# First down projection of a two-layer trunk: the B21 rows stay in SBUF, and the A12 chunks take over their buffers

## The chip, the cores and the metric

The kernel runs on one core of one Trainium2 chip. The metric is device time in microseconds (us) of one execution. Three runs before the change gave 2187.07, 2189.74 and 2186.4 us; the median is 2187.07 us.

## The reference

Two layers over 1024 tokens of width 1024, all float32. Layer 0 has an attention mixer, layer 1 a recurrent one, and each ends with a SwiGLU block. What this case touches is the end of layer 0's SwiGLU block and the start of layer 1's recurrent block:

```python
def swiglu(h, w_gate, w_up, w_down):
    return (jax.nn.silu(h @ w_gate) * (h @ w_up)) @ w_down
...
        f = swiglu(h, ffn_w_gate[layer], ffn_w_up[layer], ffn_w_down[layer])   # w_down: 2816 x 1024
        x = x + rmsnorm(f, norm_ffn_post[layer])
...
        h = rmsnorm(x, norm_mix_pre[layer])                 # of the next layer
    proj = h @ w_in                                         # recurrent_mixer: 1024 x 2048
    gate, xr = jnp.split(proj, 2, axis=-1)
```

## The kernel before

**Numbers.** Each float32 operand of a matmul is split into two fp32r parts, `hi` (a cast on ScalarE, ACT) and `lo` (source minus `hi`, on VectorE, DVE), and each product is three matmuls: hi·hi, hi·lo, lo·hi. A cast and a subtraction thus stand ahead of every operand of TensorE (PE).

**The down stage** (`down`, run once for each layer) multiplies the 1024 x 2816 activations by `w_down` with a seven-product scheme on 2 x 2 blocks. The inner dimension is cut in 11 steps, j = 0 to 10 (`NP`), of two row blocks of 128. The block row 1 of `w_down` at step j has a left half, B21, and a right half, B22. The products run in the order p1, p6, p7, p5, p4, p3, and last A12·B21. Each of the first six is 11 steps of 4 x 3 matmuls of 128 x 512 into four banks `ps`. The last is done in four **units** a = 0 to 3, each of 33 matmuls into one bank: a unit gives one group of 128 rows.

- p4 needs B21 once, to form an operand (`t4`), and the units need it again.
- p3 loads two halves of a `raw` buffer (3 buffers) for each step: S4 (a result of the stage before, stored in DRAM) and B22, and splits both: S4 into a buffer of the tag `w` (8 buffers), B22 into `wb` (4).
- The units' left operand, A12, comes in three **chunks** of 4, 4 and 3 steps for each unit, so 12 chunks, each loaded from DRAM into a buffer `act` (2 buffers) and split into a buffer `wb`.

**The norms.** After p4 four groups of rows (r = 1, a = 0 to 3; the result tiles `m2`) are complete, and after each unit one more (r = 0; `m1`). For each one a chain runs: squares on ACT (`junk`), an inverse root on GpSimd (POOL, `rs`), scaling and adding to x on DVE, squares of x on ACT, another root on POOL, scaling on ACT, then a **turn**: eight 128 x 128 transposes on PE, written in two banks `pst`, from which ACT casts `hi` and DVE subtracts `lo` into `hT`, the next stage's right operand.

**The next stage** (`recurrent`) starts with `xr([0, 1, 2])`: three 1024 x 128 pieces of `rg_w_in` are loaded into `raw`, scaled by a gain on DVE, and split into two `w` buffers each (`whi`, `wlo`). Their matmuls take first the tokens of half 0 of `hT`, then half 1. The next pieces (c = 3 and 4) are scaled on POOL, eight instructions each.

**Order.** The code is written for a tile framework that follows every buffer and puts the instructions of each engine in an order by its own estimate of the time; `behind` (which calls `issue_after`) forces an instruction to be placed after a named one. On the chip each engine takes its queue strictly in that order: an instruction that waits holds all behind it. SP's queue issues nearly all DMAs in this part of the program. A buffer of a tag with n buffers is reused n allocations later, and its new writer waits for the last reader of the old content.

The second layer's `down` runs the same code with `keep` true; there B21 and B22 stay in the buffers `ts`.

Of the kernel before, what the change touches and what calls it, by code (L numbers as in the profile page):

```python
# [8 lines left out]
F32 = mybir.dt.float32  # L9
# [3 lines left out]
ALU = mybir.AluOpType  # L13
PSUM = bass.MemoryType.PSUM

P = 128
# [83 lines left out]
class Trunk:  # L100
# [36 lines left out]
        self.last_load = self.nc.sync.dma_start(raw.rearrange("p (a b) -> p a b", a=a), src).ins  # L137
        return raw

    def split(self, src, a, b, gain=None, raw=None, pool=False):  # L140

        nc, m = self.nc, self.main
        if raw is None:
            raw = self.raw(src, a)
        if gain is not None and pool:
            for i in range(a):
                v = raw[:, i * b:(i + 1) * b]
                nc.gpsimd.tensor_scalar(v, v, gain[:, i:i + 1], 1.0, op0=ALU.mult, op1=ALU.mult)
        elif gain is not None:
            v = raw.rearrange("p (a b) -> p a b", a=a)  # L150
            nc.vector.tensor_tensor(v, v, gain.rearrange("p (a o) -> p a o", o=1).to_broadcast([P, a, b]),
                                    op=ALU.mult)
        hi = m.tile([P, 1024], F32R, tag="w", bufs=8, name=self.uid("whi"))
        lo = m.tile([P, 1024], F32R, tag="w", bufs=8, name=self.uid("wlo"))
        nc.scalar.copy(hi, raw)  # L155
        nc.vector.tensor_tensor(lo, raw, hi.bitcast(F32), op=ALU.subtract)  # L156
        return (hi.rearrange("p (a b) -> p a b", a=a),
                lo.rearrange("p (a b) -> p a b", a=a))
# [657 lines left out]
    def down(self, l, gO, x_src, x_dst, make_sink):  # L816
# [4 lines left out]
        nc, io = self.nc, self.io  # L821
        w = io["ffn_w_down"][l]
        NP = NF // 2
        tt = nc.vector.tensor_tensor

        def block(j, row, c0=0, n=D):
            return w[(2 * j + row) * P:(2 * j + row + 1) * P, c0:c0 + n]

        def split(pool, tag, bufs, src):
            t = pool.tile([P, 2, 512], F32R, tag=tag, bufs=bufs, name=self.uid("o"))  # L830
            nc.scalar.copy(t[:, 0], src)  # L831
            tt(t[:, 1], src, t[:, 0].bitcast(F32), op=ALU.subtract)  # L832
            return t

        def matmuls(ps, a, b, first, last):
            nc.tensor.matmul(ps, a[0], b[:, 0], start=first, stop=False)  # L836
            nc.tensor.matmul(ps, a[0], b[:, 1], start=False, stop=False)  # L837
            nc.tensor.matmul(ps, a[1], b[:, 0], start=False, stop=last)  # L838

        def product(operands, first=0):  # L840
            ps = [self.psum() for _ in range(4)]
# [8 lines left out]
        main = self.main  # L850

        keep = make_sink is nullcontext
        with self.pool(f"d{l}") as ap, ExitStack() as right:
# [12 lines left out]
            def fetch(name, j, src=None):  # L866
                r = main.tile([P, 2, 512], F32, tag="raw", bufs=3, name=self.uid("raw"))
                self.mark = nc.sync.dma_start(r[:, 0], gO[name][j]).ins
                if src is not None:
                    nc.sync.dma_start(r[:, 1], src)  # L870
                return r[:, 0], r[:, 1]
# [25 lines left out]
            def p5(j):  # L897
# [2 lines left out]
                    self.load(ts[j][:, 0], block(j, 1, 0, 512))  # L900
                return sp(a), sp(ts[j][:, 1])

            def p4(j):
                a, t4 = fetch("A22", j, None if keep else block(j, 1, 0, 512))
                tt(t4, ts[j][:, 2], ts[j][:, 0] if keep else t4, op=ALU.subtract)
                if keep:
                    self.load(ts[j][:, 1], block(j, 1, 512, 512))
                return sp(a), sp(t4)
# [15 lines left out]
            with make_sink() as sink:  # L924
                def norm(r, a, m):
                    ms, mg = [(slice(0, D), m)], m
                    if r == 0 and sink is None:
                        ms = [(c, m[:, c]) for c in (hi, lo)]
                        mg = ap.tile([P, D], F32, tag="mg", bufs=1, name=self.uid("mg"))

                    x = main.tile([P, D], F32, tag="raw", bufs=3, name=self.uid("x")) if keep and r == 0 else None
                    self.post_norm(ms, mg, x_src, x_dst, (r, a), gpost, sink, ap, x)

                for a in range(4):
                    norm(1, a, m2[a])

                def p3(j):
                    r = main.tile([P, 2, 512], F32, tag="raw", bufs=3, name=self.uid("raw"))
                    nc.sync.dma_start(r[:, 0], gO["S4"][j])
                    b22 = ts[j][:, 1]  # L940
                    if not keep:
                        b22 = r[:, 1]
                        nc.sync.dma_start(b22, block(j, 1, 512, 512))
                    return split(main, "w", 8, r[:, 0]), split(ap, "wb", 4, b22)

                for m, ps in zip(m1, product(p3)):
                    tt(m[:, hi], ps, m[:, hi], op=ALU.add)
                b21 = []
                for j in range(NP):
                    if keep:  # L950
                        src = ts[j][:, 0]
                    else:
                        if j % 2 == 0:
                            r = main.tile([P, 2, 512], F32, tag="raw", bufs=3, name=self.uid("raw"))
                        src = r[:, j % 2]
                        nc.sync.dma_start(src, block(j, 1, 0, 512))
                    b21.append(split(*((main, "w", 8) if j < 6 else (ap, "wc", 5)), src))
                for a in range(4):
                    ops = []
                    for j in range(0, NP, 4):  # L960
                        n = min(4, NP - j)
                        r = ap.tile([P, 4, P], F32, tag="act", bufs=2, name=self.uid("act"))[:, :n]
                        self.load(r, gO["A12"][:, j:j + n, a * P:(a + 1) * P])
                        t = ap.tile([P, 2, 4, P], F32R, tag="wb", bufs=4, name=self.uid("o"))
                        nc.scalar.copy(t[:, 0, :n], r)  # L965
                        tt(t[:, 1, :n], r, t[:, 0, :n].bitcast(F32), op=ALU.subtract)  # L966
                        ops += [(t[:, 0, i], t[:, 1, i]) for i in range(n)]
                    ps = self.psum()
                    for j in range(NP):
                        matmuls(ps, ops[j], b21[j], j == 0, j == NP - 1)  # L970
                    tt(m1[a][:, lo], ps, m1[a][:, lo], op=ALU.add)
                    norm(0, a, m1[a])
        self.mark = None


    def recurrent(self, ap, hT, yT):
# [21 lines left out]

        psum = self.psum

        def w_load(c0, pool=True):

            return self.split(w_in[:, c0:c0 + P].rearrange("(k p) c -> p k c", p=P), KT, P, self.gcol[:, 2],
                              pool=pool)

        def act(*a, **k):

# [9 lines left out]

        def xr(cs):

            ws = {c: w_load(1024 + c * P, len(cs) == 1) for c in cs}  # L1020
            carry = {c: ap.tile([P, 3], F32, tag="carry", bufs=4, name=self.uid("carry")) for c in cs}
            for c in cs:
                xcs[c] = [ap.tile([P, S], F32, tag="xc", bufs=4, name=self.uid("xc"))]
# [237 lines left out]
```

## Time and profile before

| | us |
|---|---|
| median of three runs | 2187.07 |
| the profiled execution | 2190.47 |
| its span, first to last instruction | 2188.7 |
| PE busy | 2160.6 (99%) |
| DVE busy | 1502.0 (69%) |
| ACT busy | 1171.6 (54%) |
| PE waits between 1150 and 1243 us, in which p3 and the units lie | 4.7 |

The span is the time between the first and the last instruction; the profiled execution's own time is 1.8 us longer. PE is called busy while a matmul is anywhere in its pipeline. A 128 x 512 matmul is in it for 0.39 us while the next one starts 0.227 us later, so a gap below 0.16 us does not show as a wait, and the loss is better read from the starts of matmuls. Lines (L837) are those of the kernel before; a line such as L831 (`hi`) or L832 (`lo`) belongs to a helper that all products share.

### The profile page before, as it was taken

The numbers are of one execution on the slowest core, as the hardware profiler recorded it, in microseconds if no ns is written. First come the engines' busy times: TensorE is split into PE (matmuls) and PEld (weight loads), VectorE is DVE, ScalarE is ACT, GpSimd is POOL, SyncE is SP. The second block draws the span as 40 slices with busy tenths as digits, with TensorE's granted clock in tenths as the row PEclk, the third lists the DMA queues.
The fourth block names the chain that finished last, engine by engine and source line by source line (L and its number), as shares of the span: only waits on it lengthen the run. The fifth ranks groups of instructions, "written<-read, shape, count | busy, mean of one in ns | idle before, by whom it ended". The sixth has DMA issues, their size and how long they took to land.

```text
span 2188.7 us, 30464 instructions
## 1 busy us (share of the span) xinstructions
PE 2160.6 (99%) x11140; PEld 1803.1 (82%) x11140; DVE 1502.0 (69%) x2458; ACT 1171.6 (54%) x2174; POOL 210.3 (10%) x398
## 2 busy tenths in 40 slices
PE   9999999999999999999999999999999999999998
PEld 8898989878788888888887777888788888888886
DVE  4747555556877677767768678437786767758675
ACT  6656555556855545433446676538755454424453
POOL 2111113121100000000002333102100000000011
PEclk9999999999999999999999999999999999999999
DMA  7111011126334233336468411356233333328565
GB/s 284 44 40 59 30 38 56 45 93 216 135 98 138 92 121 96 112 100 242 135 194 241 128 57 39 110 189 228 76 131 101 122 96 102 106 87 292 169 182 155
DMA packets 169039, 272.32 MB, mean 124 GB/s; under 512 B 14140, under 2 KB 95036, under 8 KB 168888
## 3 DMA queue, kind: packets, MB, share of 16 engines
q1 hardware_dynamic: 168248, 268.27, 38.3%
q10 hardware_dynamic: 640, 2.10, 0.3%
q8 instruction: 87, 1.43, 0.3%
q14 instruction: 64, 0.52, 0.1%
HBM read 202.69 MB, written 65.54 MB: 123 GB/s over the span
## 4 chain that ended last, share of the span: by engine, by line
PE 88%; DVE 4%; DMA 3%; ACT 2%; issue 2%; POOL 0%; SPq 0%; POOLq 0%; ACTq 0%; DVEq 0%
PE ps L752 13%; PE ps L753 13%; PE ps L751 13%; PE ps L594 7%; PE ps L837 5%; PE ps L838 5%; PE ps L836 5%; PE pso L366 3%; PE tr L431 3%; PE psq L166 3%; PE psq L167 2%; PE psq L168 2%; PE ps L166 2%; PE ps L167 2%; PE ps L168 2%
## 5 line engine op out<-in xcount | busy, mean ns | idle before, releaser
L752 PE MATMUL ps<-hS,q 128*128 128x512 f32 (+1 forms) x1288 | 489.8, 380 | 0.5 <-DVE hS L89 0.5
L751 PE MATMUL ps<-hS,q 128*128 128x512 f32 (+1 forms) x1288 | 490.0, 381 | 0.0
L753 PE MATMUL ps<-hS,q 128*128 128x512 f32 (+1 forms) x1288 | 489.3, 380 | 0.0
L722 DVE TENSOR_TENSOR q<-raw,q 128x512 fp32r<-128x512 f32 x308 | 205.6, 687 | 175.1 <-ACT q L721 174.3
L752 PEld LDWEIGHTS ps<-hS,q 128*128 128x128 f32 x1288 | 242.9, 189 | 47.1 <-DVE hS L89 0.9
L751 PEld LDWEIGHTS ps<-hS,q 128*128 128x128 f32 x1288 | 242.5, 189 | 46.4 <-DVE tf L89 0.5
L753 PEld LDWEIGHTS ps<-hS,q 128*128 128x128 f32 x1288 | 243.0, 189 | 45.6
L721 ACT CAST q<-raw 128x512 fp32r<-128x512 f32 x308 | 178.7, 616 | 172.5 <-DVE raw L730 116.9
L837 PE MATMUL ps<-o,o 128*128 128x512 f32 x616 | 240.2, 390 | 0.6 <-DVE o L832 0.6
L838 PE MATMUL ps<-o,o 128*128 128x512 f32 x616 | 237.9, 390 | 0.3 <-DVE o L966 0.3
L836 PE MATMUL ps<-o,o 128*128 128x512 f32 x616 | 221.6, 391 | 3.5 <-ACT o L965 3.0
L709 ACT ACTIVATE raw<-raw,gcol 128x256 f32<-128x256 f32 x352 | 150.4, 498 | 131.2 <-DMA raw<-in_ffn_w_up_dram 73.2
L831 ACT CAST o<-raw 128x512 fp32r<-128x512 f32 x184 | 110.3, 620 | 161.7 <-PE ps L838 49.4
L182 POOL TENSOR_SCALAR rs<-ss 128x1 f32<-128x1 f32 x52 | 25.2, 484 | 1420.3 <-ACT junk L178 1355.8
L832 DVE TENSOR_TENSOR o<-raw,o 128x512 fp32r<-128x512 f32 x184 | 123.5, 689 | 54.4 <-ACT o L831 53.7
L836 PEld LDWEIGHTS ps<-o,o 128*128 128x128 f32 x616 | 115.4, 188 | 30.5 <-ACT o L965 5.1
L837 PEld LDWEIGHTS ps<-o,o 128*128 128x128 f32 x616 | 115.7, 188 | 25.8 <-DVE o L832 2.1
L838 PEld LDWEIGHTS ps<-o,o 128*128 128x128 f32 x616 | 115.6, 188 | 24.8 <-DVE o L966 1.2
L156 DVE TENSOR_TENSOR wlo<-raw,whi 128x1024 fp32r<-128x1024 f32 x76 | 93.6, 1231 | 57.4 <-ACT whi L155 56.3
L419 DVE TENSOR_TENSOR_SCAN pr<-pr,zero 128x128 f32<-128x128 f32 (+7 forms) x64 | 86.6, 1358 | 51.3 <-POOL pr L416 49.6
L155 ACT CAST whi<-raw 128x1024 fp32r<-128x1024 f32 x76 | 79.7, 1049 | 48.5 <-PE ps L167 19.9
L166 PE MATMUL psq<-hT,whi 128*128 128x512 f32 x256 | 102.3, 400 | 0.2 <-DVE st L337 0.2
(206 smaller groups left out, 4263.8 us busy)
## 6 DMA issues: line engine op xcount, KB each, us to landing
raw<-in_ffn_w_gate_dram SPq DMA_DIRECT2D x44, 512.0 KB, 4.2
raw<-in_ffn_w_up_dram SPq DMA_DIRECT2D x44, 512.0 KB, 4.2
gS<-c SPq DMA_DIRECT2D x88, 256.0 KB, 3.7
raw<-gS SPq DMA_DIRECT2D x88, 256.0 KB, 2.9
gA<-c SPq DMA_DIRECT2D x66, 256.0 KB, 3.3
raw<-in_ffn_w_down_dram SPq DMA_DIRECT2D x63, 256.0 KB, 4.4
raw<-gA SPq DMA_DIRECT2D x44, 256.0 KB, 2.8
t<-in_ffn_w_down_dram SPq DMA_DIRECT2D x22, 512.0 KB, 6.6
```

The costliest lines, as they stand in the source:

```text
L166: nc.tensor.matmul(ps, wh[:, kt, cols], hh[:, kt, :], start=kt == 0, stop=False)
L594: self.matmul = nc.tensor.matmul(ps[:, n * 512:(n + 1) * 512], x, y[:, n, :], start=first and i == 0, stop=last and i == len(passes) - 1).ins
L709: nc.scalar.activation(raw[:, i], raw[:, i], AF.Copy, scale=gain[:, 4 * k + i:4 * k + i + 1])
L721: self.last = nc.scalar.copy(t[:, 0], src).ins
L722: self.last_lo = nc.vector.tensor_tensor(t[:, 1], src, t[:, 0].bitcast(F32), op=ALU.subtract).ins
L751: nc.tensor.matmul(ps, a[:, 0, kt, :], bh, start=kt == 0, stop=False)
L752: nc.tensor.matmul(ps, a[:, 0, kt, :], bl, start=False, stop=False)
L753: self.matmul = nc.tensor.matmul(ps, a[:, 1, kt, :], bh, start=False, stop=kt == 3).ins
L832: tt(t[:, 1], src, t[:, 0].bitcast(F32), op=ALU.subtract)
L836: nc.tensor.matmul(ps, a[0], b[:, 0], start=first, stop=False)
L837: nc.tensor.matmul(ps, a[0], b[:, 1], start=False, stop=False)
L838: nc.tensor.matmul(ps, a[1], b[:, 0], start=False, stop=last)
```

## The change

Only the first `down` and the start of `recurrent` change in what they do; the second `down` keeps its order on every engine.

1. In p4 the B21 rows go into 11 buffers `act` of their own and stay there. The 11 loads of B21 after p3 go away. Steps 0 to 4 are split inside p3's steps (into `wc`, 5 buffers), steps 5 to 10 after p3 (into `w`). Before, steps 0 to 5 went into `w` and 6 to 10 into `wc`.
2. The 12 A12 chunks take the same 11 buffers, each as soon as the B21 rows in it are split.
3. The turns are held. The norms are started as before, but their transposes are placed by hand: three of r = 1 at the steps 5, 7 and 9 of p3, the fourth and then those of r = 0 behind step 7 of units 0, 2 and 3, the last two behind unit 3.
4. The gain scaling of the first three `rg_w_in` pieces, c = 0, 1, 2, is placed behind the last split of unit c + 1.

```diff
-    def split(self, src, a, b, gain=None, raw=None, pool=False):
+    def split(self, src, a, b, gain=None, raw=None, pool=False, behind=()):
...
-            nc.vector.tensor_tensor(v, v, gain.rearrange("p (a o) -> p a o", o=1).to_broadcast([P, a, b]),
-                                    op=ALU.mult)
+            with self.behind(behind):
+                nc.vector.tensor_tensor(v, v, gain.rearrange("p (a o) -> p a o", o=1).to_broadcast([P, a, b]),
+                                        op=ALU.mult)
...
+            b21 = []
+
+            def small():
+                return ap.tile([P, 512], F32, tag="act", bufs=2 if keep else NP, name=self.uid("act"))
+
+            def split_b21(j, src):
+                return split(*((main, "w", 8) if (j < 6 if keep else j >= 5) else (ap, "wc", 5)), src)
+
             def p4(j):
-                a, t4 = fetch("A22", j, None if keep else block(j, 1, 0, 512))
-                tt(t4, ts[j][:, 2], ts[j][:, 0] if keep else t4, op=ALU.subtract)
+                a, t4 = fetch("A22", j)
+                b21.append(ts[j][:, 0] if keep else small())
+                if not keep:
+                    self.load(b21[j], block(j, 1, 0, 512))
+                tt(t4, ts[j][:, 2], b21[j], op=ALU.subtract)
...
-                    self.post_norm(ms, mg, x_src, x_dst, (r, a), gpost, sink, ap, x)
-
-                for a in range(4):
-                    norm(1, a, m2[a])
+                    return self.post_norm_of(ms, mg, x_src, x_dst, (r, a), gpost, sink, ap, x)(True)
+
+                turns = [norm(1, a, m2[a]) for a in range(4)]
+
+                def turn():
+                    if not keep:
+                        with self.behind([self.matmul]):
+                            turns.pop(0)()()
 
                 def p3(j):
+                    if j in (5, 7, 9):
+                        turn()
...
+                        if j < 5:
+                            b21[j] = split_b21(j, b21[j])
...
-                for j in range(NP):
-                    if keep:
-                        src = ts[j][:, 0]
-                    else:
-                        if j % 2 == 0:
-                            r = main.tile([P, 2, 512], F32, tag="raw", bufs=3, name=self.uid("raw"))
-                        src = r[:, j % 2]
-                        nc.sync.dma_start(src, block(j, 1, 0, 512))
-                    b21.append(split(*((main, "w", 8) if j < 6 else (ap, "wc", 5)), src))
+                for j in range(0 if keep else 5, NP):
+                    b21[j] = split_b21(j, b21[j])
...
-                        r = ap.tile([P, 4, P], F32, tag="act", bufs=2, name=self.uid("act"))[:, :n]
+                        r = small().rearrange("p (n b) -> p n b", n=4)[:, :n]
...
+                    self.units.append(self.last_lo)
...
                         matmuls(ps, ops[j], b21[j], j == 0, j == NP - 1)
+                        if j == 7 and a != 1:
+                            turn()
                     tt(m1[a][:, lo], ps, m1[a][:, lo], op=ALU.add)
-                    norm(0, a, m1[a])
+                    turns.append(norm(0, a, m1[a]))
+                if not keep:
+                    for t in turns:
+                        t()()
...
-            ws = {c: w_load(1024 + c * P, len(cs) == 1) for c in cs}
+            ws = {c: w_load(1024 + c * P, len(cs) == 1, () if len(cs) == 1 else self.units[c + 1:c + 2]) for c in cs}
```

How this moves instructions is shown at three places. The order's own line numbers are used: a line of the kernel after stands one to some twenty lines further down (L831 and L832 become L832 and L833, L965 becomes L978, L178 becomes L179, L212 becomes L213).

On SP, from the end of p3's loads into the units. `raw<-in_ffn_w_down` is B21, `act<-gA` an A12 chunk, `raw<-in_rg_w_in` a piece of the next stage's weight, `x` and `xs` a norm's rows in and out. Before:

```order
L956 DMA raw_11569<-in_ffn_w_down_dram 128x512 x2
L196 DMA act_11602<-gA_0_6649 128x3x128
L956 DMA raw_11578<-in_ffn_w_down_dram 128x512 x2
L196 DMA act_11675<-gA_0_6649 128x4x128
L196 DMA x_11725<-xs_89 64x1024 x2
L956 DMA raw_11587<-in_ffn_w_down_dram 128x512
L137 DMA raw_11941<-in_rg_w_in_dram 128x8x128
L196 DMA act_11680<-gA_0_6649 128x4x128
L137 DMA raw_11948<-in_rg_w_in_dram 128x8x128
L196 DMA act_11685<-gA_0_6649 128x3x128
```

After, at the end of p3's loads (`gS` is S4; the last pair is step 10):

```order
L259 DMA xs_90<-x_11220 64x1024 x2
L957 DMA raw_11529<-gS_0_10_6648 128x512
L961 DMA raw_11529<-in_ffn_w_down_dram 128x512
L137 DMA raw_11935<-in_rg_w_in_dram 128x8x128
L197 DMA x_11636<-xs_89 64x1024 x2
L137 DMA raw_11942<-in_rg_w_in_dram 128x8x128
L259 DMA xs_90<-x_11239 64x1024 x2
L197 DMA act_11665<-gA_0_6649 128x3x128
L197 DMA act_11724<-gA_0_6649 128x4x128
L197 DMA act_11729<-gA_0_6649 128x4x128
```

The B21 loads are gone, chunks stand in one run, and step 10's pair now stands behind the store of `x_11220`, the third norm's rows.

On ACT, at the end of p3. Before, `o_11520` and `o_11523` are S4 and B22 of step 10, `o_11544` is B21 of step 0 and `o_11594` the first A12 chunk:

```order
L831 CAST o_11520<-raw_11517 128x512
L212 ACTIVATE m_9920<-x_11237,rs_11250 128x1024
L831 CAST o_11523<-raw_11517 128x512
L831 CAST o_11544<-raw_11542 128x512
L57 CAST hT_11167<-pst_11223 128x4x2x64
L57 CAST hT_11167<-pst_11228 128x4x2x64
L831 CAST o_11548<-raw_11542 128x512
L178 ACTIVATE m_9921,ss_11284<-x_11270 128x1024
L965 CAST o_11594<-act_11592 128x512
```

After, `o_11532` and `o_11535` are S4 and B22 of step 10, the casts between them B21 of steps 5 to 9, `o_11574` the first chunk:

```order
L213 ACTIVATE m_9920<-x_11220,rs_11233 128x1024
L832 CAST o_11532<-raw_11529 128x512
L832 CAST o_11554<-act_11034 128x512
L832 CAST o_11557<-act_11057 128x512
L832 CAST o_11560<-act_11080 128x512
L832 CAST o_11563<-act_11103 128x512
L832 CAST o_11566<-act_11126 128x512
L832 CAST o_11535<-raw_11529 128x512
L978 CAST o_11574<-act_11572 128x512
```

Five casts of B21 have come between the two operands of p3's last step, and the chunk's cast stands right behind.

On ACT, around the end of unit 3. `whi` are the next stage's weights, `m` the norms' rows, `hT<-pst` the cast behind a turn. Before:

```order
L155 CAST whi_11951<-raw_11948 128x1024
L178 ACTIVATE junk_11811,ss_11813<-m_9916 128x1024
L965 CAST o_11853<-act_11851 128x384
L212 ACTIVATE m_9915<-x_11725,rs_11738 128x1024
L155 CAST whi_11958<-raw_11955 128x1024
L57 CAST hT_11167<-pst_11744 128x4x2x64
L155 CAST whi_12180<-raw_12178 128x1024
L57 CAST hT_11167<-pst_11749 128x4x2x64
```

After:

```order
L179 ACTIVATE junk_11791,ss_11793<-m_9916 128x1024
L156 CAST whi_11945<-raw_11942 128x1024
L179 ACTIVATE m_9916,ss_11802<-x_11788 128x1024
L156 CAST whi_11952<-raw_11949 128x1024
L57 CAST hT_11178<-pst_11847 128x4x2x64
L57 CAST hT_11178<-pst_11852 128x4x2x64
L213 ACTIVATE m_9916<-x_11788,rs_11801 128x1024
```

The squares of `x_11788`, which wait for a norm's chain on DVE and POOL, now stand ahead of the third weight's cast (`whi_11952`) and of both casts behind the turn of the group before.

More of the change, by code (lines that the diff above doesn't have):

```diff
@@ L837, in matmuls @@
             nc.tensor.matmul(ps, a[0], b[:, 1], start=False, stop=False)
-            nc.tensor.matmul(ps, a[1], b[:, 0], start=False, stop=last)
+            self.matmul = nc.tensor.matmul(ps, a[1], b[:, 0], start=False, stop=last).ins
         def product(operands, first=0):
@@ L947, in down @@
                     tt(m[:, hi], ps, m[:, hi], op=ALU.add)
-                b21 = []
-                for j in range(NP):
-                    if keep:
-                        src = ts[j][:, 0]
-                    else:
-                        if j % 2 == 0:
-                            r = main.tile([P, 2, 512], F32, tag="raw", bufs=3, name=self.uid("raw"))
-                        src = r[:, j % 2]
-                        nc.sync.dma_start(src, block(j, 1, 0, 512))
-                    b21.append(split(*((main, "w", 8) if j < 6 else (ap, "wc", 5)), src))
+                for j in range(0 if keep else 5, NP):
+                    b21[j] = split_b21(j, b21[j])
+                self.units = []
                 for a in range(4):
@@ L965, in down @@
                         nc.scalar.copy(t[:, 0, :n], r)
-                        tt(t[:, 1, :n], r, t[:, 0, :n].bitcast(F32), op=ALU.subtract)
+                        self.last_lo = tt(t[:, 1, :n], r, t[:, 0, :n].bitcast(F32), op=ALU.subtract).ins
                         ops += [(t[:, 0, i], t[:, 1, i]) for i in range(n)]
+                    self.units.append(self.last_lo)
                     ps = self.psum()
@@ L999, in recurrent, with w_load @@
         psum = self.psum
-        def w_load(c0, pool=True):
+        def w_load(c0, pool=True, behind=()):
             return self.split(w_in[:, c0:c0 + P].rearrange("(k p) c -> p k c", p=P), KT, P, self.gcol[:, 2],
-                              pool=pool)
+                              pool=pool, behind=behind)
         def act(*a, **k):
```

## Prediction

> **What bounds the kernel now.** I read the page's busy times first, then PE's waits in the stage that is changed, then PE's timeline there.
>
> ```profile
> span 2188.7 us, 30464 instructions
> PE 2160.6 (99%) x11140; PEld 1803.1 (82%) x11140; DVE 1502.0 (69%) x2458; ACT 1171.6 (54%) x2174; POOL 210.3 (10%) x398
> ```
>
> PE bounds the kernel, and the change takes no matmul away. It can only win time in which PE waits. The waits of PE, ACT and DVE between 1150 and 1243 us (what waited, for what: total, times, longest):
>
> ```profile
> PE ps L836 <- ACT o L965: 3.0, 3, 1.4
> PE pst L222 <- ACT m L212: 0.6, 2, 0.3
> PE ps L837 <- DVE o L832: 0.5, 2, 0.2
> ...
> ACT o L965 <- DMA act<-gA: 7.8, 5, 2.1
> ACT o L831 <- DMA raw<-in_ffn_w_down_dram: 4.7, 3, 2.0
> ```
>
> PE waits for the A12 chunks' casts (L965), and these wait for the chunks' DMAs; the casts of the B21 rows (L831) wait for theirs. These are what the change moves early. The waits hide part of the loss, so I count it from PE's timeline (start, duration; the first pair of transposes, the first matmuls behind it, the next stage's first matmul, its half 1):
>
> ```profile
> 1148.07 0.39 PE L836 MATMUL ps<-o,o 128*128 128x512 f32 x1
> ...
> 1152.83 0.39 PE L836 MATMUL ps<-o,o 128*128 128x512 f32 x1
> ...
> 1163.94 1.03 PE L222 MATMUL pst<-ident,m 128*128 128x128 f32 x8
> 1164.73 0.48 PE L837 MATMUL ps<-o,o 128*128 128x512 f32 x1
> ...
> 1224.50 0.84 PE L166 MATMUL ps<-hT,whi 128*128 128x512 f32 x3
> ...
> 1242.95 0.62 PE L166 MATMUL ps<-hT,whi 128*128 128x512 f32 x2
> ```
>
> From 1148.07 to 1152.83 lie 21 matmuls: 0.227 us each. An undisturbed turn costs 1164.73 - 1163.94 = 0.79. From 1164.73 to 1242.95 the program has 275 matmuls and 7 turns, so 275 x 0.2267 + 7 x 0.79 = 67.87 us would do; the trace takes 78.22. **10.35 us are lost here**, 9.8 of them before 1224.50. That is the most that the change can win.
>
> **The change part by part.**
>
> *B21 is not loaded again, chunks come early.* Eleven loads leave SP's queue. The first five chunks' loads stand among p3's loads, the other seven follow the splits of the rows whose buffers they take, all before or in unit 0. A load of a chunk and a pair's load took (us from issue to landing, min, median, max; first chunks `act`, then `raw`):
>
> ```profile
> DMA to landing us min/median/max: 3.0/4.6/6.1
> ...
> DMA to landing us min/median/max: 3.9/4.8/5.8
> ```
>
> A unit takes 33 x 0.2267 = 7.5 us, so chunks 6 to 12 are there a unit or more ahead of use: I cost the chunks at nothing, and the waits on L965 and on B21's casts go. What covers them is a unit of matmuls; without it one would cost at most the longest wait above, 1.4. The same work on DVE (27.7 + 32.3 us busy in 74.4, below) must now fit in some 65:
>
> ```profile
> 1150.11:1185.00 34.89, 34.71 (x165) 28.59 (x164) 27.68 (x38) 26.19 (x45) 11.06 (x16) 1.00 0.78 240
> 1185.00:1224.50 39.50, 34.91 (x150) 24.65 (x149) 32.29 (x43) 24.59 (x41) 7.12 (x10) 1.00 0.79 220
> ```
>
> (After each stretch: its length, PE, PEld, DVE, ACT and POOL busy, clock, DMA share, GB/s.) The five B21 splits that move ahead of p3 take 5 x 0.69 = 3.4 off (the mean of L832, below). DVE and ACT fit as a sum, but not every operand is in time. Three places remain.
>
> *End of p3.* On SP, step 10's pair now stands behind the store of the third norm's rows, which before was issued 1.9 us after the pair:
>
> ```profile
> 1168.60 0.45 SPq L939 DMA_DIRECT2D raw<-gS  x1
> 1169.09 0.43 SPq L943 DMA_DIRECT2D raw<-in_ffn_w_down_dram  x1
> 1169.85 1.11 SPq L196 DMA_DIRECT2D x<-xs  x2
> 1171.00 1.23 SPq L258 DMA_DIRECT2D xs<-x  x2
> ...
> 1173.74 1.13 ACT L831 CAST o<-raw 128x512 fp32r<-128x512 f32 x2
> ```
>
> The store waits for DVE's sum (L256), which I leave where it was. So S4 is issued at 1171.00 + 1.23 = 1172.2 and lands 4.8 later, 1177.0. Its cast, five of B21 and B22's cast follow at 0.52 each (two took 1.13 with their overlap), 7 x 0.52 + 0.1 = 3.75: 1180.75. Without a wait PE would want B22 after 120 matmuls and two turns from p3's start (61 matmuls before 1163.94, so 1150.11): 1150.11 + 27.2 + 1.58 = 1178.9. The wait is 1.9; with landings of 3.9 and 5.8, 1.0 to 2.9. I take 1.9, from the median. The first chunk's cast is 0.5 behind and PE needs it 0.9 later: free.
>
> *End of unit 3.* The next stage's `whi`, `wlo` of c = 1 and 2 take the `w` buffers of B21 steps 5 to 8, read until the middle of unit 3; before, those of steps 0 to 3. Then the ACT queue holds the third `whi` and both casts of a turn behind the squares of x of unit 2's norm. That chain, by these rows:
>
> ```profile
> L256 DVE SCALAR_TENSOR_TENSOR x<-m,rs,x 128x1024 f32<-128x1024 f32 x8 | 10.3, 1282 | 4.4 <-POOL rs L183 4.2
> L178 ACT ACTIVATE m<-x 128x1024 f32<-128x1024 f32 x8 | 8.5, 1062 | 7.8 <-DVE x L256 7.8
> L57 ACT CAST hT<-pst 128x512 fp32r<-128x512 f32 x16 | 8.8, 581 | 1.8 <-PE pst L222 1.8
> L155 ACT CAST whi<-raw 128x1024 fp32r<-128x1024 f32 x4 | 4.2, 1047 | 0.0
> L156 DVE TENSOR_TENSOR wlo<-raw,whi 128x1024 fp32r<-128x1024 f32 x4 | 5.0, 1250 | 0.3 <-ACT whi L155 0.3
> L832 DVE TENSOR_TENSOR o<-raw,o 128x512 fp32r<-128x512 f32 x27 | 18.0, 687 | 3.8 <-ACT o L831 3.7
> ...
> 1212.15 0.19 ACT L178 ACTIVATION_READ_ACCUMULATOR junk<-m 128x1 f32 x1
> ...
> 1214.66 1.28 DVE L256 SCALAR_TENSOR_TENSOR x<-m,rs,x 128x1024 f32<-128x1024 f32 x1 [0.46 <-POOL rs L183]
> ```
>
> Let unit 3 start at 0. The turn inside unit 2 ends six matmuls, 1.4, earlier; its casts (0.58 each) come behind another row's squares and end at some 0.35 (an estimate), DVE's two lo parts at 1.1 and unit 2's sum at 1.75. Squares (1.05 + 0.19) end at 3.0, the root reaches DVE 2.3 later (1212.34 to 1214.66): 5.3, adding to x 6.6, squares of x 7.8, third `whi` 8.85, first `hT` cast 9.4. PE wants that at 33 x 0.2267 + 0.79 = 8.3: a wait of 1.1 at most, 0.75 if the chain runs 0.35 tighter. Then DVE does the third `wlo` (1.22) before the turn's `lo` (0.6): 8.85 + 1.25 + 0.65 = 10.75, against PE at 10.1: 0.6 more. I take 1.5. Bounds: 0, if the chain is 2 us shorter; 2.5, if DVE comes to unit 2's sum a lo part and an add later.
>
> *The last turn.* Its root stands on POOL behind the scaling of c = 3 and 4:
>
> ```profile
> 1224.89 3.76 POOL L148 TENSOR_SCALAR raw<-raw,gcol 128x128 f32<-128x128 f32 x8 [2.87 <-DVE wlo L156]
> ...
> 1231.60 3.82 POOL L148 TENSOR_SCALAR raw<-raw,gcol 128x128 f32<-128x128 f32 x8 [1.99 <-DMA raw<-in_rg_w_in_dram]
> ...
> 1220.49 0.38 SPq L137 DMA_DIRECT2D raw<-in_rg_w_in_dram  x1
> ...
> 1224.57 0.80 SPq L137 DMA_DIRECT2D raw<-in_rg_w_in_dram  x1
> ```
>
> Before, the second piece started 1231.60 - 1224.57 = 7.0 after its load's issue, and the last turn lost 0.55 from 1224.50 on (18.45 against 72 x 0.2267 + 2 x 0.79). These loads wait for `raw` buffers that the late `wlo` of c = 1 and 2 set free, so relative to PE they are issued some 1 to 3 us later. Against that, the first scaling need not wait 2.87 for DVE's `wlo` as before. I take a wait of 1.0, between 0 and 2.2.
>
> *Slower pace behind each wait*: 0.1 for each of three, 0.3, by this step of 0.34 instead of 0.227:
>
> ```profile
> 1191.94 0.50 PE L836 MATMUL ps<-o,o 128*128 128x512 f32 x1 [0.82 <-ACT o L965]
> 1192.28 0.40 PE L837 MATMUL ps<-o,o 128*128 128x512 f32 x1
> ```
>
> **Sum.** Remaining loss 1.9 + 1.5 + 1.0 + 0.3 = 4.7; won 10.35 - 4.7 = 5.65. The profiled execution took 2190.47 (span 2188.7 and 1.8 around it), 3.4 above the median of the runs; it would take 2184.8. On the median: 2187.07 - 5.65 = **2181.4**. The ends together, 1.0 and 7.9, give 2177.7 and 2184.6.
>
> **Rivals.**
>
> *No new wait.* If the norm's chain and step 10's pair come in time, 9.4 to 10.35 are won: 2177.2. For it: none of PE's waits above is for an operand of p3 (the two on L832 are B21's, in unit 0). Against: the order puts five casts between one step's operands.
>
> *DVE takes back the gain, or step 10's pair lands late.* S4's slowest landing in this stretch was 7.4:
>
> ```profile
> DMA to landing us min/median/max: 2.5/4.3/7.4
> ```
>
> Then the first wait is 4.5 instead of 1.9 and 3 are won: 2184.0. Nearly the same follows if DVE, 56.6 us of work in 65, makes every second of p3's 11 steps wait 0.5. DMA share of 0.78 speaks for it, the eleven loads that leave against it. By the Trainium skill, "TensorE: Matmul & The Clock Gate", Part 1, an idle window of some 3.4 us halves the PE clock; the trace has 1.00 throughout with waits up to 1.4, so no run here shows that yet, and a wait of 4.5 would be the place for it.
>
> *Slower: the last turn's root is starved on POOL.* One square-sum step on POOL took 1.25 beside DVE's scaling (1205.03 to 1206.26) and 0.22 alone:
>
> ```profile
> 1205.03 1.23 DVE L250 TENSOR_TENSOR m<-m,g 128x1024 f32<-128x1024 f32 x1 [0.62 <-ACT junk L178]
> ...
> 1205.09 1.25 POOL L182 TENSOR_SCALAR rs<-ss 128x1 f32<-128x1 f32 x1 [22.86 <-ACT junk L178]
> ...
> 1211.38 0.22 POOL L182 TENSOR_SCALAR rs<-ss 128x1 f32<-128x1 f32 x1 [4.39 <-ACT m L178]
> ```
>
> If each of the sixteen scalings waits out a DVE instruction, they take 16 x (1.25 - 0.47) = 12.5 longer, all of it in front of the last turn: 5.65 - 12.5 = -6.9, so 2193.9. It decides from a stretch of 5.65 on. For it: DVE is denser now. Against: the two groups of eight took 3.76 and 3.82, though `wlo` ran beside the first. The Trainium skill, "SBUF — State Buffer", Who interferes with whom, has the rule: a DVE instruction with two SBUF inputs and a POOL instruction that reads SBUF shut each other out for a whole instruction. By that rule 2193.9 could come; the row of 1.25 agrees with it, the rows of 3.76 and 3.82 show little of it.
>
> **How the numbers follow.** Some 0.2% (4.4 us) is what a measurement can tell from no change. My forecast, 4.4 to 8 won, has 0.52; no new wait 0.14; the late pair or DVE, within 0.2%, 0.26; slower 0.08. Faster is thus 0.66, same 0.26, slower 0.08. The range runs from 2177.2, the first rival, to 2186.0, where 1 us is won, between the second rival and none; outside lie the slower case and a rest.
>
> **What would show it.** In the profile after: PE's waits on L978 (L965 before) between p3 and the next stage are gone; a wait of 1 to 3 us for a cast (L832) at p3's last step; one of 0.5 to 2.5 at the next stage's first matmuls on `hT`; one at the last turn; 67.9 + 4.7 us from the first turn to half 1. Wrong would be waits on the chunks again, a slow clock in p3, or a turn in the units that waits for its norm (I gave them 4 us of slack).

## The result, and the profile after

| | before | after |
|---|---|---|
| median of 20 runs, us | 2186.91 (2184.28 to 2189.74) | 2183.47 (2179.94 to 2186.96) |
| ratio, 95% interval | | 0.9986 (0.998 to 0.9992) |
| profiled execution, span, us | 2190.47, 2188.7 | 2183.28, 2181.5 |
| p3's first matmul to half 1, us | 1150.11 to 1242.95: 92.84 | 1149.03 to 1237.95: 88.92 |
| of it lost | 10.35 | 6.43 |

The kernel became 3.4 us faster (1.7 to 4.4 by the interval), not the 5.65 forecast. The last two rows are the measure that I use from here on: from p3's first matmul to half 1 stand 336 matmuls and 8 turns, 336 x 0.2267 + 8 x 0.79 = 82.49 us without a wait; what the trace takes beyond that is lost. The traces give 10.35 - 6.43 = 3.92 won in this stage. The two spans differ by 7.2, since the rest of two executions of the same code differs by some microseconds. A second trace of the changed kernel took 90.15 in the stage (below), so one reading is good to about 1.2 us.

Three views of the kernel after follow: the busy time, PE's waits from 1135 to 1245 us (what waited, for what: total, times, longest), and the rows of PE's timeline around which it lost time. All rows in this section are of the kernel after; its lines are one further down than before's, and some 13 to 20 in p3 and the units.

```profile
PE 2155.4 (99%) x11140; PEld 1802.7 (83%) x11140; DVE 1498.4 (69%) x2458; ACT 1169.1 (54%) x2174; POOL 207.6 (10%) x398
```

```profile
PE ps L837 <- ACT o L832: 2.6, 2, 1.4
PE ps L167 <- ACT hT L57: 0.8, 1, 0.8
PE ps L168 <- DVE hT L58: 0.4, 1, 0.4
PE ps L838 <- DVE o L833: 0.2, 1, 0.2
```

```profile
1149.03 0.39 PE L837 MATMUL ps<-o,o 128*128 128x512 f32 x1
...
1159.75 0.39 PE L839 MATMUL ps<-o,o 128*128 128x512 f32 x1
1161.40 1.19 PE L837 MATMUL ps<-o,o 128*128 128x512 f32 x4 [1.26 <-ACT o L832]
1162.75 0.50 PE L838 MATMUL ps<-o,o 128*128 128x512 f32 x1 [0.16 <-DVE o L833]
...
1179.86 0.39 PE L839 MATMUL ps<-o,o 128*128 128x512 f32 x1
1181.62 1.42 PE L837 MATMUL ps<-o,o 128*128 128x512 f32 x5 [1.37 <-ACT o L832]
...
1217.75 0.39 PE L839 MATMUL ps<-o,o 128*128 128x512 f32 x1
1218.96 0.98 PE L167 MATMUL ps<-hT,whi 128*128 128x512 f32 x3 [0.82 <-ACT hT L57]
1220.34 0.50 PE L168 MATMUL ps<-hT,whi 128*128 128x512 f32 x1 [0.40 <-DVE hT L58]
...
1236.38 1.03 PE L223 MATMUL pst<-ident,m 128*128 128x128 f32 x8
...
1237.95 0.84 PE L167 MATMUL ps<-hT,whi 128*128 128x512 f32 x3
```

The waits for the chunks' casts (L965 before, 3.0 us; L978 now) are gone, and no turn waits. Three places remain. At p3's step 4 the gap is 1161.40 - 1159.75 - 0.23 = 1.42, with 0.32 more at the step's first matmul on a lo part (1162.75): 1.74. At step 10 it is 1.53. At the next stage's first matmuls it is 0.98 + 0.56 = 1.54. The other 1.62 are many small delays of 0.01 to 0.12.

What PE waits for is seen on the other engines. The rows are of step 4 (ACT), step 10 (SP's queue, then ACT) and the end of unit 3 (ACT, then DVE):

```profile
1158.65 1.06 ACT L179 ACTIVATE m<-x 128x1024 f32<-128x1024 f32 x1 [3.32 <-DVE x L257]
...
1159.70 1.04 ACT L179 ACTIVATE junk<-m 128x1024 bf16<-128x1024 f32 x1
...
1160.74 1.12 ACT L832 CAST o<-raw 128x512 fp32r<-128x512 f32 x2
```

```profile
1171.80 1.23 SPq L259 DMA_DIRECT2D xs<-x  x2
1173.13 0.89 SPq L957 DMA_DIRECT2D raw<-gS  x1
1174.06 1.24 SPq L961 DMA_DIRECT2D raw<-in_ffn_w_down_dram  x1
...
1177.82 0.62 ACT L832 CAST o<-raw 128x512 fp32r<-128x512 f32 x1 [1.07 <-DMA raw<-gS]
1178.35 2.70 ACT L832 CAST o<-act 128x512 fp32r<-128x512 f32 x5
1180.95 0.61 ACT L832 CAST o<-raw 128x512 fp32r<-128x512 f32 x1
```

```profile
1216.34 1.06 ACT L179 ACTIVATE m<-x 128x1024 f32<-128x1024 f32 x1 [1.40 <-DVE x L257]
...
1217.40 1.03 ACT L156 CAST whi<-raw 128x1024 fp32r<-128x1024 f32 x1
1218.34 1.06 ACT L57 CAST hT<-pst 128x512 fp32r<-128x512 f32 x2
...
1218.46 1.23 DVE L157 TENSOR_TENSOR wlo<-raw,whi 128x1024 fp32r<-128x1024 f32 x1 [1.02 <-ACT whi L156]
1219.61 0.68 DVE L58 TENSOR_TENSOR hT<-pst,hT 128x512 fp32r<-128x512 f32 x1
```

In all three, an operand that is there stands in an in-order queue behind something that is not, or not yet needed. The casts of B22 for steps 4 and 5 (1160.74) stand behind squares of x that waited 3.32 for DVE. Step 10's two casts have five of B21 between them. The casts of the turn (1218.34) stand behind squares that waited 1.40 and a third `whi`.

### The profile page after: what moved, and what is told of

The parts are those of the page before. It is cut to its first block, busy times and chain, and to the rows that moved or that the text cites. A ratio compares the mean times of both kernels' runs of the same rounds, so it can differ in the third digit from the quotient of the medians.

```text
span 2181.5 us, 30430 instructions
## 1 busy us (share of the span) xinstructions
PE 2155.4 (99%) x11140; PEld 1802.7 (83%) x11140; DVE 1498.4 (69%) x2458; ACT 1169.1 (54%) x2174; POOL 207.6 (10%) x398
## 4 chain that ended last, share of the span: by engine, by line
PE 89%; DVE 4%; DMA 2%; ACT 2%; issue 1%; POOL 0%; SPq 0%; POOLq 0%; DVEq 0%; ACTq 0%
PE ps L753 13%; PE ps L754 13%; PE ps L752 13%; PE ps L595 8%; PE ps L838 5%; PE ps L839 5%; PE ps L837 5%; PE pso L367 3%; PE tr L432 3%; PE psq L167 3%; PE psq L168 3%; PE psq L169 2%; PE ps L168 2%; PE ps L169 2%; PE ps L167 2%
## 5 line engine op out<-in xcount | busy, mean ns | idle before, releaser
L832 ACT CAST o<-raw 128x512 fp32r<-128x512 f32 x173 | 103.9, 620 | 148.0 <-PE ps L839 56.5
L833 DVE TENSOR_TENSOR o<-raw,o 128x512 fp32r<-128x512 f32 x173 | 115.9, 687 | 51.9 <-ACT o L832 51.2
```

## Experiments

Stage time and loss come from one trace of each kernel, the ratio to the kernel before from some 6 to 12 runs.

| run | stage, us | lost | ratio (95%) |
|---|---|---|---|
| after, again | 90.15 | 7.66 | 0.9989 (0.9973 to 1.0004) |
| scaling not held | 91.63 | 9.14 | 1.0008 (0.9999 to 1.0017) |
| chunks' loads behind p3 | 89.07 | 6.58 | 0.9968 (0.9956 to 0.998) |
| before + chunk buffers | 96.65 | 14.16 | 1.0029 (1.0018 to 1.0039) |
| rows loaded again | 95.39 | 12.90 | 1.0004 (0.9994 to 1.0014) |
| two chunk buffers | 95.81 | 13.32 | 1.0009 (0.9999 to 1.002) |
| B21 behind p3 | 88.68 | 6.19 | 0.9983 (0.9974 to 0.9992) |
| norms inside p3 | 91.36 | 8.87 | 0.9993 (0.9984 to 1.0003) |
| unit 3's order | 87.23 | 4.74 | 0.9984 (0.9972 to 0.9997) |
| three edits | 87.05 | 4.56 | 0.9979 (0.9965 to 0.9994) |
| + first chunk first | 86.12 | 3.63 | 0.9965 (0.9954 to 0.9975) |
| + gates' wlo held | 85.77 | 3.28 | 0.9973 (0.9963 to 0.9983) |

The times follow the stage, with up to some 3 us of difference (chunks' loads behind p3: 3.8 less in the stage, 7.0 by the ratio, and why is not shown). The verdicts below therefore rest on the waits. Each expectation names its theories, and the sentence behind it says which one came.

**The same kernel again.**

> The changed kernel once more, to see how far one trace of it stands from another. If the stage's time is a property of the order of instructions, p3's first matmul to half 1 takes 88.9 within 0.4 (6.0 to 6.9 lost), with the same three waits (step 4, step 10, next stage's first matmuls). If what differs between the runs so far is chance in the DMA's landings, it moves by 1 us or more, and the experiments' stage times must be read with that in mind.

The three places are the same: 1.68 at step 4, 1.96 at step 10, 1.55 at the next stage. A fourth wait, 0.57 for DVE (L933, a result of the product before), came early in p3. So the places are properties of the order, but the loss moved by 1.2 and not by 0.4: sums that differ by less are not told apart, the waits themselves are.

### Undoing one part at a time

**The held turns.** Written without that part, the program comes out with the same instructions in the same order and with the same waits on all five engines. The hold is worth nothing here, and there is no run for it.

**The held scaling.** Of the changed kernel, one argument is emptied:

```diff
-ws = {c: w_load(1024 + c * P, len(cs) == 1, () if len(cs) == 1 else self.units[c + 1:c + 2]) for c in cs}
+ws = {c: w_load(1024 + c * P, len(cs) == 1, ()) for c in cs}
```

> The changed kernel with one part undone: the next stage's three scalings on DVE are not held behind the units' lo parts. From p3's first matmul to half 1 the kernel before took 92.84 us, of which 336 matmuls and 8 turns need 82.49, so it lost 10.35; the changed kernel took 88.92 and lost 6.43. Theory A (the gain is from the chunk buffers and the kept rows, the hold is worth little): the scalings run while DVE has room, the stage loses 6.4 to 7.0. Theory B (the hold is needed): three scalings of 1.22 stand on DVE ahead of lo parts of B21 and of the chunks in unit 0, PE waits there for DVE (L833, L979) for 1 us or more, and the stage loses 7.5 to 10. Time after A: as the changed kernel, 3 to 4 below before; after B: 0 to 2.5 below.

Theory B came in the stage (9.14), and by the time (1.0008) no gain is left at all. On DVE the scaling of c = 0 waits for its load and stands ahead of lo parts of B21 and of the last B22 (DVE, then PE):

```profile
1180.49 1.23 DVE L152 TENSOR_TENSOR raw<-raw,gcol 128x1024 f32<-128x1024 f32 x1 [0.85 <-DMA raw<-in_rg_w_in_dram]
1181.63 1.89 DVE L833 TENSOR_TENSOR o<-act,o 128x512 fp32r<-128x512 f32 x3
1183.44 0.69 DVE L833 TENSOR_TENSOR o<-raw,o 128x512 fp32r<-128x512 f32 x1
...
1184.18 0.50 PE L838 MATMUL ps<-o,o 128*128 128x512 f32 x1 [2.19 <-DVE o L833]
```

**When the chunks are loaded.**

```diff
-nc.sync.dma_start(r[:, 0], gO["S4"][j])
+s4 = nc.sync.dma_start(r[:, 0], gO["S4"][j]).ins
+if not keep:
+    self.mark = s4
```

Loads that are written later stay behind `mark`.

> The changed kernel with the chunks' loads held behind the load of p3's last pair; they still have eleven buffers. Theory A (what counts is that a chunk need not wait for a buffer; the queue is free enough): the first chunk's load is issued at some 1175 and lands 4.6 to 6.5 later, 1180 to 1182, when PE ends p3; PE waits up to 1 us for it and not for a later one, since five loads are issued in 4 us and a unit takes 7.5; the stage loses 6.4 to 7.5, and S4 of p3's last steps comes no later. Theory B (the loads must stand among p3's): waits for the chunks at each of the first units, 1 us or more each as before the change (3.0 in three waits), the stage loses 9 or more.

Theory A came in its number (6.58), and PE waited for no chunk. But the waits are others: step 4's is gone, and at p3's end PE waited 2.13 for a lo part and then ran slowly (last section). The early loads are worth nothing by themselves.

**The chunk buffers alone**, in the kernel before:

```diff
-r = ap.tile([P, 4, P], F32, tag="act", bufs=2, name=self.uid("act"))[:, :n]
+r = ap.tile([P, 4, P], F32, tag="act", bufs=2 if keep else NP, name=self.uid("act"))[:, :n]
```

> The kernel before with one thing alone: the A12 chunks have eleven buffers of their own in place of two, and B21's rows are loaded again as before. Theory A (the chunks' two buffers were what cost): PE's waits for L965 are gone, the stage loses 4.5 to 6.5 in place of 10.35, as much as the whole change gives. Theory B (the eleven second loads must go too): the chunks are there, but the B21 rows' casts wait for their DMA as before (4.7 us in three waits on ACT), unit 0's last rows come at some 1191 to 1194 where PE would want them at 1189, PE waits there 1 to 4 us, and the stage loses 7.5 to 10.

This has theory B's sign and is worse than both: 14.16 are lost, and by the time the kernel is slower than before. Two turns now come close together at unit 3's end; the second needs the PSUM banks of the first, whose lo parts stand on DVE behind three `wlo` and a norm:

```profile
1225.04 1.11 PE L222 MATMUL pst<-ident,m 128*128 128x128 f32 x4 [4.38 <-DVE hT L58]
```

**All but the kept rows** (loads and splits of B21 behind p3 as before the change, the rest changed):

```diff
...
+if not keep:
+    if j % 2 == 0:
+        r = main.tile([P, 2, 512], F32, tag="raw", bufs=3, name=self.uid("raw"))
+    src = r[:, j % 2]
+    nc.sync.dma_start(src, block(j, 1, 0, 512))
+b21[j] = split_b21(j, src)
...
```

> The changed kernel with one part undone: B21's rows are loaded a second time and split behind p3, as before the change; the chunks have eleven buffers, the scalings and the turns are held. The run with the chunk buffers alone lost 14.16 (4.5 of it where a turn waited for the lo part of the turn ahead of it on DVE, 1.4 and 0.9 at casts). Theory A (the kept rows are needed for the gain, since otherwise DVE's splits of eleven rows crowd unit 0 and the turns and the next stage's splits crowd unit 3): no wait for a chunk's DMA, but the wait for a turn's lo part stays at 2 to 4.5, and the stage loses 9 to 13. Theory B (the holds were what that run lacked): the stage loses 6 to 7.5, as the changed kernel.

Theory A came in size (12.90), not in place: the worst wait is for a chunk's cast, which stood on ACT behind a row's cast whose load was late (ACT, then PE):

```profile
1190.72 0.62 ACT L832 CAST o<-raw 128x512 fp32r<-128x512 f32 x1 [3.22 <-DMA raw<-in_ffn_w_down_dram]
1191.25 0.61 ACT L980 CAST o<-act 128x512 fp32r<-128x512 f32 x1
...
1191.91 0.80 PE L837 MATMUL ps<-o,o 128*128 128x512 f32 x1 [2.61 <-ACT o L980]
```

**All but the chunk buffers**:

```diff
-with make_sink() as sink:
+with make_sink() as sink, self.pool(f"ch{l}") as ch:
...
-r = small().rearrange("p (n b) -> p n b", n=4)[:, :n]
+r = ch.tile([P, 4, P], F32, tag="act2", bufs=2, name=self.uid("act"))[:, :n]
```

> The changed kernel with the kept rows, but the chunks in two buffers of their own as before the change, not in B21's eleven. (The allocation moves some instructions of a later stage, so it is read by the stage, not by the time.) Theory A (two buffers are what made the chunks late): a chunk's load is issued when the chunk two ahead of it has been split, takes 4.6 to 6.5 to land and 1.2 to be split, so that two chunks come in 6 to 8 us where PE uses three in 7.5: PE waits for chunks in each unit, 4 to 8 us in all, and the stage loses 8 to 12. Theory B (the eleven second loads were what made them late): with these gone the two buffers do, and the stage loses 6 to 7.

The loss is above theory A's 8 to 12, and not by its path: PE waited for no chunk at all. ACT waited for chunks' DMAs, and what paid was the norm behind them. Below are ACT's largest wait from 1150 to 1244 us, and a place (ACT, then PE) where the squares of a row stand behind a chunk's cast, so that its turn comes 2.09 late:

```profile
ACT o L978 <- DMA act<-gA: 13.4, 6, 4.3
```

```profile
1203.55 0.52 ACT L978 CAST o<-act 128x384 fp32r<-128x384 f32 x1 [4.26 <-DMA act<-gA]
1203.97 1.06 ACT L179 ACTIVATE m<-x 128x1024 f32<-128x1024 f32 x1
...
1206.56 1.15 ACT L213 ACTIVATE m<-x,rs 128x1024 f32<-128x1024 f32 x1 [0.93 <-POOL rs L184]
...
1207.76 1.13 PE L223 MATMUL pst<-ident,m 128*128 128x128 f32 x8 [2.09 <-ACT m L213]
```

So three parts carry the gain, and only together: without the held scaling 9.14 are lost, without the rows 12.90, without the buffers 13.32, with all 6.43 and 7.66, with the buffers alone 14.16, with none 10.35. By the time, none of the three that lack one part is faster than the kernel before (1.0008, 1.0004 and 1.0009).

### Taking away what is left

**Step 10: B21's rows 5 to 10 split behind the last pair.** The splits of rows j >= 5 get `behind=self.last_split`, the cast and lo part of step 10's B22.

> The changed kernel with the splits of B21's rows 5 to 10 held behind the casts and lo parts of p3's last pair. Theory A (the five casts stand between the last step's two operands, B22 having landed at 1174.06 + 5.0 = 1179.1): the wait of 1.4 at p3's end goes to 0 to 0.3; the five casts now stand ahead of the first chunk's, so 0.3 to 0.6 may come back there; the stage loses 5.2 to 5.9 in place of 6.43. Rival (the load is what is late, because the pair stands behind the store of the third norm's rows): the wait stays at 1.0 or more and the loss at 6.2 to 6.6.

Theory A came at step 10: there is no wait, so the five casts were what held it, not the load. 0.75 came back at the first chunk (0.59 for DVE, L983), whose cast now stands behind theirs. The sum, 6.19, lies between the two theories (up to 5.9, from 6.2).

**Step 4: the norms' sum, store and squares written inside p3**, behind steps 4, 6, 8 and 9 (`rests.pop(0)(True)` in `p3`).

> The changed kernel, but the sum, store and squares of x of the r = 1 norms are written inside p3, behind its steps 4, 6, 8 and 9, so that B22's casts of steps 4 and 5 stand ahead of the squares of x on ACT. Theory A (the squares, which wait 3.3 us for DVE's sum, hold these casts): the 1.74 lost at step 4 goes to 0 to 0.2, the raw buffers come free earlier and step 10's pair with them, so the wait at p3's end falls too; the stage loses 3.8 to 4.8 in place of 6.43. Rival 1 (the cast waits for its own buffer or its load): 1.3 or more stays. Rival 2: the norms are now too late, and a turn waits 1 to 3 us for its scaled row, or the first chunk's cast, which stands behind the squares of the fourth row, is late at p3's end; the loss stays at 6 or more.

Step 4's wait is gone: the squares did hold the casts. But rival 2 decided. The rows' loads went behind as well, DVE waited for one, and the second turn waited for the first one's lo part on DVE (rows below: DVE, then PE). At the next stage's first matmul PE waited 2.03, with a slow pace behind it (last section).

```profile
1174.25 1.28 DVE L257 SCALAR_TENSOR_TENSOR x<-m,rs,x 128x1024 f32<-128x1024 f32 x1 [1.95 <-DMA x<-xs]
...
1176.06 1.28 DVE L58 TENSOR_TENSOR hT<-pst,hT 128x512 fp32r<-128x512 f32 x2
...
1176.80 1.26 PE L223 MATMUL pst<-ident,m 128*128 128x128 f32 x8 [2.04 <-DVE hT L58]
```

**End of unit 3: the rows whose buffers the next stage takes are read first** (the chunks' order changes likewise).

```diff
...
+js = list(range(NP))
+if not keep and a in (3,):
+    js = js[4:] + js[:4]
-for j in range(NP):
+for j in js:
...
```

> The changed kernel, but unit 3 takes B21's rows in the order 4 to 10, then 0 to 3 (its chunks likewise), so that the buffers which the next stage's whi and wlo of c = 1 and 2 take come free some 2 to 3 us earlier. Theory A (those buffers are what makes the end of unit 3 late): the third whi and the casts of unit 3's turn no longer stand behind the squares of x, the wait at the next stage's first matmuls (0.98 + 0.56) goes to 0 to 0.4, the stage from p3 to half 1 loses 5.0 to 5.5 in place of 6.43. Rival: the norm's chain sets it (squares waiting for DVE's sum), the wait stays at 1.2 or more. Second rival: eight scalings on POOL now stand ahead of the second root of unit 2's norm, and a turn in the next stage waits 0.5 to 3, which takes the gain back or more.

Theory A came: the casts of the turn stand ahead of the squares, PE's wait for them (0.98) is gone and 0.57 for DVE is left; the turns on the far side did not wait. The stage goes from 6.43 to 4.74, but not all of this is the edit's: at step 4, which it does not touch, the gap is 0.85 in place of 1.42. By the time (0.9984 against 0.9986) no gain shows.

**Together.**

> Three edits together: the chunks' loads behind p3's last pair, B21's rows 5 to 10 split behind the last pair's casts and lo parts, unit 3 in the order 4 to 10, 0 to 3. In the run with the loads alone, step 4's wait was gone, and at p3's end PE waited 2.13 for DVE (the lo part of the last B22 stood behind three lo parts of B21), followed by steps of 0.43 us in place of 0.23 that cost 1.9 more. Theory A: with the three lo parts out of the way the last B22's lo part comes 1.8 earlier, PE waits 0.2 to 0.6 there, keeps its pace, and at the next stage's first matmuls it waits 0.4 to 0.6; the stage loses 2.2 to 3.2, and the time is 3.3 to 4.2 below the changed kernel's, 6.5 to 8 below before's. Rival: the edits collide (the first chunk's cast stands behind the squares of the fourth row, which wait for the row's load), PE waits 1 to 2.5 us there, and the stage loses 5 to 7.

> The same three edits, and the first chunk is split ahead of B21's rows 5 to 10, which unit 0 needs later than it. Theory A: as the three edits or up to 0.5 better, the stage loses 2.0 to 3.2. Rival: unit 0's last rows are late now, PE waits 0.5 to 1.5 for them (L833), and the stage loses more than with the three edits.

With the three edits p3's end lost 0.35 and the turn behind it 0.61, about what theory A had. But a new wait of 1.99 came at the next stage, where I had 0.4 to 0.6, so the loss is 4.56, between theory and rival, and the time is some 4.6 below before's, not 6.5 to 8. With the first chunk first it is 3.63, above theory A's 3.2: the rest of the stage lost 1.3, and that one wait is all that counts (DVE, then PE):

```profile
1215.22 2.35 DVE L157 TENSOR_TENSOR wlo<-raw,whi 128x1024 fp32r<-128x1024 f32 x2
1217.49 1.28 DVE L58 TENSOR_TENSOR hT<-pst,hT 128x512 fp32r<-128x512 f32 x2
...
1218.22 0.50 PE L168 MATMUL ps<-hT,whi 128*128 128x512 f32 x1 [2.19 <-DVE hT L58]
```

> The run before (three edits, first chunk first) and one edit more: of the gates' weights, which the next stage needs only after its first projections, the wlo is held on DVE behind the lo parts of unit 3's turn. In the run before, PE lost 2.34 where the next stage's first matmul on hT's lo part waited for DVE, which did two wlo in a row (2.35) first. Theory A: one wlo of 1.17 less stands ahead, PE waits 0.8 to 1.2 there in place of 2.19, nothing else moves, the stage loses 2.3 to 2.8 in place of 3.63, and the time is 6.5 to 10 below before's. Rival: the wait is the cast's on ACT (behind the squares of x), and stays at 1.8 or more.

Half of theory A came: one `wlo` less stands ahead, and the wait is 1.60, not 0.8 to 1.2, because the first `wlo` still does (DVE, 1215.17 to 1216.30), and PE came 0.7 earlier against it. The stage lost 3.28, the least of all. By the time the last two kernels are at 0.9965 (0.9954 to 0.9975) and 0.9973 (0.9963 to 0.9983). Both are faster than the kernel before; the first also lies clear of the changed kernel (0.998 to 0.9992), the second just touches it. The run with only the chunks' loads behind p3 is as fast, 0.9968 (0.9956 to 0.998), so which of the three is the best stays open.

## Why the prediction was right or wrong

- **The bound and the count.** These were right. The stage was PE's, the chunks' waits were lost time, and the loss at stake was 10.35.
- **Chunks at nothing.** This was right: there is no wait on L978. The chunks landed later than I took (4.6), but ahead of use. The last figure is the median from issue to landing, from 1139 to 1240 us:

```profile
act<-gA SPq DMA_DIRECT2D x8, 256.0 KB, 6.2
```

- **End of p3, 1.9 (1.0 to 2.9).** This was right in size and place: 1.53, and 1.96 in the second trace. The mechanism, five casts between the pair's, is shown by their removal. The size is partly luck: counted from p3's first matmul, S4 was issued 2.0 later than I took (1173.13 - 1149.03 = 24.1, against 22.1), and PE came 2.3 later, 1.74 of it lost at step 4. The two nearly cancel.
- **End of unit 3, 1.5 (0 to 2.5).** This was right: 1.54, in the parts forecast (1.1 at most for the cast, 0.6 for DVE; 0.98 and 0.56 measured). It is shown by the run with unit 3's order.
- **The last turn, 1.0 (0 to 2.2).** This was wrong; it did not wait. The row was scaled at 1233.69 + 1.15 = 1234.84, PE came at 1236.38:

```profile
1223.01 3.78 POOL L148 TENSOR_SCALAR raw<-raw,gcol 128x128 f32<-128x128 f32 x9 [4.56 <-DVE wlo L157]
...
1227.20 2.45 POOL L148 TENSOR_SCALAR raw<-raw,gcol 128x128 f32<-128x128 f32 x7
...
1233.69 1.15 ACT L213 ACTIVATE m<-x,rs 128x1024 f32<-128x1024 f32 x1 [1.01 <-POOL rs L184]
```

  The second piece did not wait for its load, as I had it, but went straight on behind the first.
- **Slower pace, 0.3.** This was too small: 1.62 are left beside the three places.
- **What failed: step 4.** The sum had no term for it. I followed the casts of p3's last step only. That "none of PE's waits above is for an operand of p3" held for the order of before, and the change reorders ACT within p3: in the new order ACT does the squares of x, which wait for DVE, ahead of B22's casts of steps 4 and 5, and this cost 1.74. The run with the norms inside p3, in which these casts stand ahead of the squares, lost nothing at step 4.
- **The sum.** 4.7 forecast, 6.43 measured: -0.4 (step 10), 0 (unit 3), -1.0 (last turn), +1.3 (pace), +1.7 (step 4).
- **The rivals.** "Late pair" had the time (2184.0), not the mechanism: S4 landed in 4.7. "Slower" did not come: the sixteen scalings took 3.78 + 2.45 us, 0.39 each. I had read the 3.76 and 3.82 of before as hardly stretched. That was a misreading, because such a row merges eight or nine scalings and its mean hides the one that counts: one scaling of each group took 1.33 and 1.39, beside a DVE instruction that reads two SBUF tiles, and the other fourteen 0.37 each. The first row is of before, where DVE's `wlo` ran from 1224.99 for 1.34; the other two are of after:

```profile
1225.24 1.33 POOL L148 TENSOR_SCALAR raw<-raw,gcol 128x128 f32<-128x128 f32 x1
```

```profile
1222.56 1.22 DVE L251 TENSOR_TENSOR m<-m,g 128x1024 f32<-128x1024 f32 x1
...
1223.01 1.00 POOL L148 TENSOR_SCALAR raw<-raw,gcol 128x128 f32<-128x128 f32 x1 [4.56 <-DVE wlo L157]
```

  After, one scaling of the sixteen met such an instruction and took 1.00; the other fifteen took 0.37 each, also those beside two of DVE's `lo` parts, which read one of their inputs from PSUM. The last `wlo` had ended before, since POOL waited for it. By the rule of the Trainium skill, "SBUF — State Buffer", Who interferes with whom, a scaling that meets a DVE instruction with two SBUF inputs is stretched; these rows agree with it. So the rival's mechanism exists, and what it lacked was the sixteen meetings.

## What to carry to other kernels

An operand that comes earlier only helps if nothing late stands ahead of its consumer in an in-order queue: after moving a load, walk each engine's queue and ask what every waiting instruction has behind it. Waits that PE's own list names need not name the cause: with two buffers PE waited for no chunk, and the chunks were the cause all the same, through the norm behind them on ACT. Judge parts of a change together with what they lean on: the buffers alone were slower than nothing, and one part (the held turns) was already what the scheduler did.

## What was unexpected in the hardware

A wait of PE of about 2 us or more can have a second price. In seven of the ten such waits in this stage, over all runs, the matmuls behind it started every 0.43 us in place of 0.23. The profile gives the granted clock, the share of full speed that TensorE's clock was allowed: behind these seven waits it is 0.50, for 3.41 or 6.83 us, and 1.00 in the rest of the stage. The waits followed by it were 2.03, 2.09, 2.13, 2.19, 2.61, 2.91 and 4.38; 1.99, 2.04 and a second 2.19 were not, nor any of 1.80 or less.

The length of the wait alone thus does not decide. What sorts all ten is a grid of windows: within each trace, the points at which the clock changes lie whole multiples of 3.41 us apart. With that grid laid over the stage, the clock fell from 1.00 to 0.50 behind every window in which PE was idle for 2.02 us or more (2.02, 2.09, 2.13, 2.19, 2.37, 2.45 and 3.41), and behind no other; the largest idle time without that price was 1.90. The two on either side of the bound are from the run with the norms inside p3 and the one with three edits (stretches of time: length, PE, PEld, DVE, ACT and POOL busy, granted clock, DMA share, GB/s; the idle time is the length less PE's busy time):

```profile
1219.56:1222.97 3.41, 1.39 (x5) 0.87 (x6) 2.39 (x4) 3.41 (x7) 0.79 (x2) 1.00 0.92 221
1222.97:1226.39 3.42, 3.42 (x10) 2.65 (x9) 3.10 (x4) 1.76 (x3) 1.28 (x2) 0.50 0.95 250
```

```profile
1217.34:1220.75 3.41, 1.51 (x7) 0.93 (x5) 3.41 (x5) 1.62 (x3) 0.20 (x1) 1.00 0.98 249
1220.75:1224.16 3.41, 3.31 (x15) 2.75 (x16) 2.13 (x4) 1.15 (x2) 3.24 (x9) 1.00 0.95 257
```

The 2.04 and the second 2.19 fell across an edge: 0.43 and 1.61, and 0.84 and 1.35, in their two windows. In the first pair of rows two waits of one window, 1.61 of the 2.03 and another of 0.41, add up to the 2.02. The halved clock lasted a second window where PE was idle for 0.55 to 1.02 within the first (three times), and one window where it was not (four times).

The price is half of the time that PE works at the halved clock: 0.5 x 3.41 = 1.7 us for one window. With two chunk buffers, one window behind the wait of 2.09 (1.7) and 1222.87 to 1229.15 behind that of 2.91 (0.5 x 6.28 = 3.1) make up some 4.8 of the 13.32 lost. One such window, at 1548 us in a later stage, is in before's trace and not in after's: 1.7 of the 7.2 us by which the two spans differ. That no run showed such a clock yet, as the prediction has it, was thus true of the stage alone. So in this stage a wait below 1.9 cost itself unless another fell into the same window, and a longer one could cost about twice itself. The bound between 1.90 and 2.02 is of this stage and its 128 x 512 matmuls: near 445 us, among shorter ones, 1.64 idle in a window of the changed kernel's trace was enough.

The Trainium skill, "TensorE: Matmul & The Clock Gate", Part 1, has the halved clock and ties it to an idle window of some 3.4 us that runs freely. The grid of 3.41 us agrees with a free-running window; that a window idle for 2.02 of its 3.41 us was enough differs from a window that must be idle throughout, and here the measurement decides.
